# Turning normed head outputs from float32r copies, one step later in the program

## The chip, the cores and the metric

The kernel runs on one core of one Trainium2 chip. A core has TensorE (matrix products; PE in the profile, its weight loads PEld), VectorE (DVE), ScalarE (ACT), GpSimd (POOL) and SyncE (SP). POOL and SP do little here but issue transfers (DMA); each has a queue and issues in order. The metric is device time in microseconds (us) of one execution, as the median of several.

## The reference, cut to what matters

The model is a trunk of two layers over 256 latent and 256 context tokens. Layer 0 has an mLSTM mixer with 4 heads, layer 1 a latent attention; each is followed by a gated convolutional FFN. The change lies in the mixer of layer 0. Its last step norms each head by itself and multiplies by the output matrix:

```python
def out(h_in, s):
    Bq, T, _ = h_in.shape
    o = jax.nn.sigmoid(h_in @ w_og).reshape(Bq, T, M_HEADS, M_DV)
    hsum = o * s.transpose(0, 2, 1, 3).astype(h_in.dtype)
    return _head_rms_norm(hsum, norm_g) @ w_out
```

Here `s` is the output of the two-way scan, per head 512 tokens by 512 columns. The kernel computes the scan of a head in closed form: a matrix W of decay weights (exponentials of gate sums plus a mask) times the scores q k, normed by row, and then times the values.

## The kernel before

All products that matter are made in float32r from split operands: a number is a high part (rounded to float32r) and a low part (the rest), and `mm3` (L427 on) issues three matmuls, high x high (L430), high x low (L433) and low x high (L434), of 128x128 weights and up to 512 columns. Weights stream from DRAM: SP loads a `raw` tile, ACT casts it (L345), DVE makes the low part (L368); three `w` buffers are in turn.

The mixer goes over the heads h = 0 to 3. In each turn `w_qk(h)` projects q and k of head h on TensorE: 4 output tiles, each of two weight units, 24 matmuls a unit, 192 in all. Beside it run *generators*, pieces of Python that emit some instructions at each step; after each unit two steps are taken (`tick`). For h of 2 and 3 these are, one after the other, `post(h - 2)` and `head(h - 1)`:

- `head` loads two gate rows spread over all partitions (`aB`, two transfers on POOL), issues two transfers that start the sums of FFN weights (`t4d`), adds the mask (`Am`, DVE, L1050), and in three groups makes W: exponentials on ACT (L1087), products with the scores on DVE (L1088), norming (L1094 to L1105). Then TensorE turns W (`PT`, 12 transposes, L1118), and ACT and DVE split the result.
- `post` norms the finished output `oh` of the head two before (tiles `tt`): squares on ACT (L1188), root, four multiplications on DVE (L1192). Then TensorE turns them: 16 transposes of 128x128 against the identity, in float32 (`hnT`, L1198), and ACT (L1205) and DVE (L1206) make the split `hn` that the output product reads.

After the projection `av` multiplies the turned W by the values, and `s_mm` makes the next scores. `v_load` loads values (`vr`) and output gates (`oh`) of the head on POOL. The output product `outmm` of the first tokens runs beside `head(3)` and `post(2)`.

The generators set only which instruction is emitted when, and so the place of each tile in its pool and the issue order of POOL's transfers. A scheduler then orders the instructions of each engine by priority and estimated readiness; a tile's wait for its buffer is put in as a semaphore. Tiles of 2 KB a partition share one pool (`s2`) of 15 buffers: `aB`, `Am`, W, `vr`, `oh` and, newly, `rr` are among them.

Of the kernel before, what the change touches and what calls it, by code (L numbers as in the profile page):

```python
# [7 lines left out]
F32 = mybir.dt.float32  # L8
F32R = mybir.dt.float32r
I32 = mybir.dt.int32  # L10
AF = mybir.ActivationFunctionType
ALU = mybir.AluOpType
# [21 lines left out]
NB, NRAW, NU, NS = 3, 3, 31, 15  # L34
# [366 lines left out]
class K:  # L401
# [73 lines left out]
    def setup(self):  # L475
        nc, p = self.nc, self.pool
        a = self.a
        self.sm = p.tile([128, a["sm"].shape[1]], F32, name="sm")
        self.sm0 = p.tile([128, NSM0], F32, name="sm0")
        jp = p.tile([128, 128], I32, tag="s2", name="jp", bufs=NS)  # L480
        nc.gpsimd.iota(jp, pattern=[[1, 128]], base=0, channel_multiplier=-1)
        self.jp = jp
        self.ident = p.tile([128, 128], F32, name="ident")
        self.mask = p.tile([128, 2, 128], F32, name="mask")
        self.k1 = p.tile([128, 1], F32, name="k1")
        nc.vector.memset(self.k1, 1.0)
        self.zero = p.tile([128, 512], F32R, tag="s2", name="zero", bufs=NS)
        nc.vector.memset(self.zero.bitcast(F32), 0.0)
        self.keps = p.tile([128, 1], F32, name="keps")
        nc.vector.memset(self.keps, EPS)  # L490
        self.cond = p.tile([128, 8, 32], F32, tag="s2", name="cond", bufs=NS)
        nc.gpsimd.memset(self.cond, 0.0)
        self.mod0 = p.tile([128, 2, 8, 2], F32, name="mod0")
        self.modc = {(0, c): self.mod0[:, c] for c in range(2)}
        self.gd = {}
        self.adav = p.tile([128, 32], F32, name="adav")
        nc.vector.memset(self.adav, 0.0)
        for l in range(2):
            for c in (3, 4) if l == 0 else (0, 1, 3, 4):
                self.modc[l, c] = p.tile([128, 8, 2], F32, name="mod%d%d" % (l, c))  # L500
            for c in (2, 5):
                self.gd[l, c] = self.dr.tile([2, D], F32, name="gd%d%d" % (l, c))
# [102 lines left out]
    def start_up(self):  # L605
# [47 lines left out]
        with self.tc.manual_schedule(engines={e.PE, e.DVE, e.Activation}):  # L653
            for _ in range(WARM):
                nc.tensor.matmul(idle, self.zero[:, 0:128], self.zero, start=True, stop=True)
            for step in STEPS:
                op, n = step[0], [int(x) for x in step[1:]]
                g = n[0]
                if op == "Q":
                    nc.scalar.activation(self.cond[:, :, 0:2], self.smc("cond").rearrange("p (a b) -> p a b", b=2),  # L660
                                         AF.Silu)
                    nc.vector.tensor_scalar(self.ident, self.jp, 0.0, None, op0=ALU.is_equal)
                    b1 = self.smc("ada_b")[:, 8:16]
                    nc.vector.tensor_scalar(b1, b1, 1.0, None, op0=ALU.add)
                elif op == "M":
                    nc.vector.tensor_scalar(self.mask[:, 0], self.jp, 0.0, NEG, op0=ALU.is_gt, op1=ALU.mult)
                    nc.vector.tensor_scalar(self.mask[:, 1], self.jp, 0.0, NEG, op0=ALU.is_lt, op1=ALU.mult)
                    self.jp = None
                elif op == "I":
                    for _ in range(g):  # L670
                        nc.tensor.matmul(idle, self.zero[:, 0:128], self.zero, start=True, stop=True)
                elif op in "Aab":
                    if g not in rows:
                        rows[g] = self.ps("adar")
                    self.ada_mm(rows[g], [(x, raw["a%d%d" % (g, x)]) for x in {"A": (0, 1), "a": (0,), "b": (1,)}[op]])
                elif op == "C":
                    adas[g] = self.ada_copy(rows[g])
                elif op == "T":
                    self.ada_T(rows[g], adas[g])
                elif op == "O":  # L680
                    self.ada_cols(g, rows[g])
                elif op == "E":
                    self.mod_tile(g)
                elif op == "H":
                    h = hT[g] = self.u("hT")
                    self.split(h[:, 0, :], h[:, 1, :], self.xT[g])
                elif op == "e":
                    h = hT[g] = self.u("hT")
                    x, (c, l) = self.xT[g], (slice(0, 256), slice(256, 512))
                    sh, sc = self.modc[0, 0][:, g], self.modc[0, 1][:, g]  # L690
                    nc.vector.tensor_scalar(x[:, c], x[:, c], sc[:, 1:2], sh[:, 1:2], op0=ALU.mult, op1=ALU.add)
                    nc.scalar.activation(h[:, 0, l], x[:, l], AF.Identity, bias=sh[:, 0:1], scale=sc[:, 0:1])
                    nc.vector.tensor_copy(h[:, 0, c], x[:, c])
                elif op == "l":
                    nc.vector.tensor_scalar(x[:, l], x[:, l], sc[:, 0:1], sh[:, 0:1], op0=ALU.mult, op1=ALU.add)
                    nc.vector.tensor_sub(h[:, 1], x, h[:, 0])
                elif op in "WwvyzKkU":
                    if op == "U":
                        g = "u"
                        raw["wu"] = raw["u0"]  # L700
                    if g not in w:
                        w[g] = [self.pool.tile([128, CW], F32R, tag="u", name="w0", bufs=NU) for _ in range(2)]
                    c = slice(256, nw) if op in "yz" else slice(0, 256 if op in "wv" else 768 if op == "U" else nw if g < 2 else 512)
                    hi, lo, src = w[g][0][:, c], w[g][1][:, c], raw["w%s" % g][:, c]
                    if op == "w":
                        nc.vector.tensor_copy(hi, src)
                    elif op in "WyKU":
                        nc.scalar.copy(hi, src)
                    if op in "WvzkU":
                        nc.vector.tensor_sub(lo, src, hi)  # L710
                else:
                    k, m = n
                    if m not in ps:
                        ps[m] = self.ps("up")
                    wk, o = (w["u"], k - 2) if m == 4 and k > 1 else (w[k], m)
                    c = slice(o * 128, (o + 1) * 128)
                    for i, j in {"V": ((0, 0), (0, 1), (1, 0)), "P": ((0, 0),), "L": ((1, 0),), "R": ((0, 1),)}[op]:
                        nc.tensor.matmul(ps[m], wk[i][:, c], hT[k][:, j], start=made[m] == 0, stop=made[m] == 23)  # L718
                        made[m] += 1
# [460 lines left out]
        self.PT = self.vh = self.oh = None  # L1180
        return r

    def post(self, h, tt):
        nc = self.nc
        ss = self.tiny(4, "ss")
        jk = self.s2("jk")
        for t in range(4):
            nc.scalar.activation(jk, tt[t], AF.Square, accum_out=ss[:, t:t + 1])  # L1188
        nc.scalar.activation(ss, ss, AF.Sqrt, bias=self.keps, scale=1.0 / 512.0)
        nc.vector.reciprocal(ss, ss)  # L1190
        for t in range(4):
            nc.vector.tensor_scalar(tt[t], tt[t], ss[:, t:t + 1], None, op0=ALU.mult)  # L1192
        yield
        g = self.smc("mng")
        for e in range(4):
            pt = self.ps("hnT")
            for t in (2, 0, 1, 3):
                q = nc.tensor.transpose(pt[:, t * 128:(t + 1) * 128], tt[t][:, e * 128:(e + 1) * 128], self.ident)  # L1198
                if e or t != 2:
                    self.behind(q, [lead])  # L1200
                else:
                    lead = q
            k = h * 4 + e
            u = self.u("hn")
            nc.scalar.activation(u[:, 0], pt, AF.Copy, scale=g[:, k:k + 1])  # L1205
            nc.vector.scalar_tensor_tensor(u[:, 1], pt, g[:, k:k + 1], u[:, 0], op0=ALU.mult, op1=ALU.subtract)  # L1206
            self.hn[k] = u
        yield


    def bcast(self, row, name):
        ts = []
# [969 lines left out]
def build(tc, off, a, out):  # L2182
    es = ExitStack()
    with es:
        k = K(tc, es, off, a)
        nc = k.nc
# [16 lines left out]
        for h in range(H0):  # L2203
# [1 line left out]
            if h == 0:  # L2205
                gens.append(k.gate_chain())
            if h >= 2:
                gens.append(k.post(h - 2, tt))
            if h >= 1:
                gens.append(k.head(h - 1, S))  # L2210
            k.bg = gens
            k.w_qk(h, 2, (lambda: k.v_load(h - 1)) if h >= 1 else None)
# [4 lines left out]
        k.xc = None  # L2217
        hn = lambda i: (k.hn[i][:, 0], k.hn[i][:, 1])
        pc = k.acc4()
        k.bg = [k.head(3, S, True), k.post(2, tt)]  # L2220
        vs = k.v_steps(3)
        for i in range(8):
            k.outmm("mout", range(i, i + 1), hn, pc, 0, 16, 2, n2=ADA_M)
            next(vs, None)
        k.drain()
        tt = k.av(3)
        k.bg = [k.post(3, tt)]
        k.outmm("mout", range(8, 12), hn, pc, 0, 16, 1, n2=ADA_M)
        k.drain()
        tokr = a["tok"].rearrange("(t p) d -> t p d", p=128)  # L2230
# [132 lines left out]
```

## Time and profile before

| | us |
|---|---|
| median of 3 runs | 1347.13 (1346.78 to 1347.27) |
| profiled execution, span from first to last instruction | 1345.3 |
| what lies around the span, against the median | 1.8 |
| TensorE busy | 1334.9 |
| DVE busy | 1059.0 |
| ACT busy | 711.7 |
| first of the two changed stretches: matmuls of `w_qk(2)` from | 458.2 |
| second: matmuls of `w_qk(3)`, its hnT at | 524.25 |

A row of the timeline gives the start, the duration, engine, line, operation and tiles (out<-in); a bracket at the end gives the idle time before it and who ended it. On TensorE the records of neighbouring matmuls overlap, so its pace is read from starts. The granted TensorE clock is 0.998 of full speed over the span.

### The profile page before, as it was taken

To read this page: it belongs to the slowest core of one execution; us is meant where nothing else is said; L and a number is where in the kernel's file an instruction comes from. 1 tells how busy PE (TensorE), PEld (TensorE's weight loads), DVE (VectorE), ACT (ScalarE), POOL (GpSimd) and SP (SyncE) were. 2 spreads that over 40 slices of the span, in tenths; PEclk is the share of its full clock that TensorE was granted. 3 is DMA by queue.
4 is the path that set the end of the run, shared out by engine and by line. 5 is a ranking of instruction groups with operands and counts; after the bars stand their busy time and mean duration, and the time that the engine had idled before them with its cause. 6 is when DMAs were issued, how large, how long until landed. Compare 5 with 4: busy or idle time off the path is not lost.

```text
span 1345.3 us, 18750 instructions
## 1 busy us (share of the span) xinstructions
PE 1334.9 (99%) x6659; PEld 1120.2 (83%) x6659; DVE 1059.0 (79%) x1745; ACT 711.7 (53%) x1252; POOL 141.5 (11%) x236
## 2 busy tenths in 40 slices
PE   9999999999999999999999999999999999999997
PEld 5777888888888888888898888888888998988886
DVE  4798656678688696897979977758899889898874
ACT  4765444445744546474644334333566767676660
POOL 0222000011101011020002011111000002000100
PEclk9999999999999999999999999999999999999999
DMA  9988848889686384776628989967866437376750
GB/s 364 330 277 279 281 163 248 233 272 307 235 281 230 102 255 149 228 292 222 215 86 261 328 260 286 282 181 184 300 223 194 157 104 219 127 212 189 263 189 32
DMA packets 99885, 304.02 MB, mean 226 GB/s; under 512 B 12312, under 2 KB 25112, under 8 KB 99712
## 3 DMA queue, kind: packets, MB, share of 16 engines
q1 hardware_dynamic: 62992, 218.65, 48.6%
q0 software_dynamic: 26000, 66.75, 17.9%
q10 hardware_dynamic: 10800, 17.44, 3.6%
q8 instruction: 52, 0.85, 0.3%
q14 instruction: 41, 0.34, 0.1%
HBM read 272.21 MB, written 42.12 MB: 234 GB/s over the span
## 4 chain that ended last, share of the span: by engine, by line
PE 97%; DMA 1%; DVE 1%; ACT 0%; issue 0%; SPq 0%; DVEq 0%; ACTq 0%
PE fin L1503 8%; PE tok L430 6%; PE tok L434 6%; PE tok L433 6%; PE fin L433 6%; PE fin L434 6%; PE y L433 6%; PE fin L430 6%; PE y L434 6%; PE y L430 6%; PE qk L430 4%; PE qk L433 4%; PE qk L434 4%; PE up L718 2%; PE up L430 2%; PE up L434 1%
## 5 line engine op out<-in xcount | busy, mean ns | idle before, releaser
L368 DVE TENSOR_TENSOR w<-raw,w 128x1024 fp32r<-128x1024 f32 (+2 forms) x286 | 343.2, 1203 | 131.9 <-ACT w L345 129.7
L345 ACT CAST w<-raw 128x1024 fp32r<-128x1024 f32 (+2 forms) x286 | 296.2, 1037 | 282.4 <-PE tok L434 77.8
L544 DVE SCALAR_TENSOR_TENSOR junk<-ar,bc 128x1024 f32<-128x1024 f32 x128 | 156.1, 1219 | 5.2 <-ACT bc L586 2.3
L433 PE MATMUL fin<-h,w 128*128 128x512 f32 (+1 forms) x370 | 139.6, 377 | 0.0
L430 PE MATMUL fin<-h,w 128*128 128x512 f32 (+1 forms) x370 | 139.5, 377 | 0.0
L434 PE MATMUL fin<-h,w 128*128 128x512 f32 (+1 forms) x370 | 139.3, 377 | 0.0
L1503 PE MATMUL fin<-h,w 128*128 128x512 f32 (+1 forms) x636 | 111.1, 337 | 0.0
L1503 PEld LDWEIGHTS fin<-h,w 128*128 128x128 f32 x636 | 97.6, 190 | 13.2
L430 PE MATMUL qk<-xc,w 128*128 128x512 f32 x256 | 100.2, 391 | 0.0
L434 PE MATMUL qk<-xc,w 128*128 128x512 f32 x256 | 99.8, 390 | 0.0
L433 PE MATMUL qk<-xc,w 128*128 128x512 f32 x256 | 99.6, 389 | 0.0
L433 PEld LDWEIGHTS fin<-h,w 128*128 128x128 f32 x370 | 69.6, 188 | 13.0
L430 PEld LDWEIGHTS fin<-h,w 128*128 128x128 f32 x370 | 69.6, 188 | 12.9
L434 PEld LDWEIGHTS fin<-h,w 128*128 128x128 f32 x370 | 69.6, 188 | 12.6
L434 PEld LDWEIGHTS qk<-xc,w 128*128 128x128 f32 x256 | 48.0, 188 | 10.1
L430 PEld LDWEIGHTS qk<-xc,w 128*128 128x128 f32 x256 | 48.1, 188 | 9.8
L433 PEld LDWEIGHTS qk<-xc,w 128*128 128x128 f32 x256 | 48.1, 188 | 9.8
L430 PE MATMUL tok<-w,hT 128*128 128x512 f32 x128 | 49.9, 390 | 0.0
L433 PE MATMUL tok<-w,hT 128*128 128x512 f32 x128 | 49.8, 389 | 0.0
L434 PE MATMUL tok<-w,hT 128*128 128x512 f32 x128 | 49.8, 389 | 0.0
L735 ACT ACTIVATE fg<-fg 128x512 f32<-128x512 f32 (+1 forms) x44 | 23.1, 525 | 50.0 <-DVE fg L733 43.9
L368 DVE TENSOR_TENSOR wu<-raw,wu 128x1024 fp32r<-128x1024 f32 (+1 forms) x37 | 43.8, 1203 | 3.5 <-ACT wu L345 3.2
(486 smaller groups left out, 3125.7 us busy)
## 6 DMA issues: line engine op xcount, KB each, us to landing
raw<-in_ws SPq DMA_DIRECT2D x282, 512.0 KB, 4.5
ar<-in_adaT SPq DMA_DIRECT2D x80, 512.0 KB, 6.0
t4d<-in_ws POOLq DMA_DIRECT2D x20, 512.0 KB, 9.1
adaw<-in_ada SPq DMA_DIRECT2D x16, 512.0 KB, 8.0
zr<-fd ACTq DMA_DIRECT2D x33, 128.0 KB, 4.6
xmd<-xr POOLq DMA_DIRECT2D x16, 256.0 KB, 4.4
xcd<-cv POOLq DMA_DIRECT2D x16, 256.0 KB, 4.9
xs<-xmd POOLq DMA_DIRECT2D x16, 256.0 KB, 6.0
```

The costliest lines, as they stand in the source:

```text
L345: self.cast = k.nc.scalar.copy(h[:, :cols], src)
L368: i = self.k.nc.vector.tensor_sub(l[:, :n], src, h[:, :n])
L430: q = mm(out, w[0], x[0], start=start, stop=False, skip_group_check=on)
L433: mm(out, w[0], x[1], start=False, stop=False, skip_group_check=on)
L434: mm(out, w[1], x[0], start=False, stop=stop, skip_group_check=on)
L544: nc.vector.scalar_tensor_tensor(o, w, 1.0, self.bc[j], op0=ALU.mult, op1=ALU.mult, accum_out=col[:, k, j:j + 1])
L718: nc.tensor.matmul(ps[m], wk[i][:, c], hT[k][:, j], start=made[m] == 0, stop=made[m] == 23)
L735: nc.scalar.activation(tmp[:, :n], tmp[:, :n], AF.Silu)
L1503: self.nc.tensor.matmul(ps[:, 0:256] if x else ps, w[x][:, k * 128:(k + 1) * 128], h[:, 0:256] if x else h, start=i == 0 and not k0, stop= ...
```

## The change

For heads 0 and 1 (`post(0)` beside `w_qk(2)`, `post(1)` beside `w_qk(3)`) each normed tile is copied, as it is, by a transfer on POOL's queue into a float32r tile `rr`; the 16 transposes then read `rr` against an identity in float32r and write float32r. `post` has one more empty step before its transposes, for heads 2 and 3 too, which keep the float32 transposes. `around` interleaves the two generators: the norm and the copies of `post`, then the first part of `head` (`aB`, `t4d`, `Am`), then the transposes of `post`, then the rest of `head`.

```diff
+        self.identr = p.tile([128, 128], F32R, name="identr")
...
+                    nc.vector.tensor_scalar(self.identr, self.jp, 0.0, None, op0=ALU.is_equal)
...
-    def post(self, h, tt):
+    def post(self, h, tt, copy=True):
...
+        rr = []
         for t in range(4):
             nc.vector.tensor_scalar(tt[t], tt[t], ss[:, t:t + 1], None, op0=ALU.mult)
+            if copy:
+                r = self.pool.tile([128, 512], F32R, tag="s2", name="rr", bufs=NS)
+                nc.gpsimd.dma_start(r.bitcast(F32), tt[t])
+                rr.append(r)
+        src, ident, dt = (rr, self.identr, F32R) if copy else (tt, self.ident, F32)
+        yield
         yield
...
-                q = nc.tensor.transpose(pt[:, t * 128:(t + 1) * 128], tt[t][:, e * 128:(e + 1) * 128], self.ident)
+                q = nc.tensor.transpose(pt[:, t * 128:(t + 1) * 128].bitcast(dt), src[t][:, e * 128:(e + 1) * 128], ident)
...
+    def around(self, post, head):
+
+        next(post)
+        yield
+        next(head)
+        yield
+        yield from post
+        yield from head
...
             if h >= 2:
-                gens.append(k.post(h - 2, tt))
-            if h >= 1:
+                gens.append(k.around(k.post(h - 2, tt), k.head(h - 1, S)))
+            elif h >= 1:
                 gens.append(k.head(h - 1, S))
...
-    k.bg = [k.head(3, S, True), k.post(2, tt)]
+    k.bg = [k.head(3, S, True), k.post(2, tt, False)]
...
-        k.bg = [k.post(3, tt)]
+        k.bg = [k.post(3, tt, False)]
```

On three engines the order moves. Line numbers of the new kernel are higher by 1 to 18; the buffer numbers behind a name differ between the two.

POOL's queue, from the gates (`oh`) of head 0 to those of head 1. Before:

```order
L1139 DMA oh<-od 128x512 x4
L1045 DMA aB_3990<-ad 128x512
L1045 DMA aB_3991<-ad 128x512
L1662 DMA t4d<-in_ws 16x8192 x2
L1133 DMA vr<-vd 128x512 x4
L1139 DMA oh<-od 128x512 x4
```

Now:

```order
L1141 DMA oh<-od 128x512 x4
L1198 DMA rr<-oh 128x512 x4
L1047 DMA aB_3931<-ad 128x512
L1047 DMA aB_3932<-ad 128x512
L1680 DMA t4d<-in_ws 16x8192 x2
L1135 DMA vr<-vd 128x512 x4
L1141 DMA oh<-od 128x512 x4
```

The four copies stand ahead of the `aB` and `t4d` of head 1.

DVE at the norm of head 0, beside the second weight unit of `w_qk(2)`. Before:

```order
L1050 TENSOR_TENSOR Am_3996<-aB_3990,mask 128x512
L1050 TENSOR_TENSOR Am_3997<-aB_3991,mask 128x512
L1190 RECIPROCAL ss<-ss 128x4
L1192 TENSOR_SCALAR oh<-oh,ss 128x512 x4
L1088 SCALAR_TENSOR_TENSOR W_4042,den<-W_4042,S 128x128
L368 TENSOR_TENSOR w<-raw,w 128x1024
L1206 SCALAR_TENSOR_TENSOR hn<-hnT,sm,hn 128x512 x4
L1088 SCALAR_TENSOR_TENSOR W_4043,den<-W_4043,S 128x256
```

Now:

```order
L1192 RECIPROCAL ss<-ss 128x4
L1195 TENSOR_SCALAR oh<-oh,ss 128x512 x4
L368 TENSOR_TENSOR w<-raw,w 128x1024
L545 SCALAR_TENSOR_TENSOR junk,adav<-ar,bc 128x1024 x2
L1052 TENSOR_TENSOR Am_3937<-aB_3931,mask 128x512
L368 TENSOR_TENSOR w<-raw,w 128x1024
L1052 TENSOR_TENSOR Am_3938<-aB_3932,mask 128x512
L1215 SCALAR_TENSOR_TENSOR hn<-hnT,sm,hn 128x512 x4
L445 TENSOR_TENSOR qk<-qk 128x512
L1090 SCALAR_TENSOR_TENSOR W_4052,den<-W_4052,S 128x128
```

`Am`, which reads `aB`, went from ahead of the norm to behind two products of the modulation (`junk`), with a weight split, `hn` and a `qk` split between it and the first W.

TensorE after 120 of the 192 matmuls of `w_qk(2)`. Before:

```order
L1118 MATMUL PT<-ident,W_4042 128x128
L1118 MATMUL PT<-ident,W 128x128 x2
L1118 MATMUL PT<-ident,W_4064 128x128 x2
L1118 MATMUL PT<-ident,W 128x128 x2
L1118 MATMUL PT<-ident,W_4064 128x128 x2
L430 MATMUL qk<-xc,w 128x512
```

Now:

```order
L1120 MATMUL PT<-ident,W_4052 128x128
L430 MATMUL qk<-xc,w 128x512
L433 MATMUL qk<-xc,w 128x512
L434 MATMUL qk<-xc,w 128x512
L430 MATMUL qk<-xc,w 128x512
L433 MATMUL qk<-xc,w 128x512
L1120 MATMUL PT<-ident,W 128x128 x2
L1120 MATMUL PT<-ident,W_4074 128x128 x2
L1120 MATMUL PT<-ident,W 128x128 x2
L1120 MATMUL PT<-ident,W_4074 128x128 x2
L434 MATMUL qk<-xc,w 128x512
```

Eight of the 12 transposes of W stand five matmuls behind the first four. The 16 transposes hnT stood after 30 matmuls of `w_qk(2)` and stand after 48. The same moves are in `w_qk(3)`. In the output product the 16 transposes of `post(2)` stand 12 matmuls later.

## Prediction

> **What bounds the kernel now.** I read the page first: its busy shares and the chain that ended last.
>
> ```profile
> span 1345.3 us, 18750 instructions
> PE 1334.9 (99%) x6659; PEld 1120.2 (83%) x6659; DVE 1059.0 (79%) x1745; ACT 711.7 (53%) x1252; POOL 141.5 (11%) x236
> PE 97%; DMA 1%; DVE 1%; ACT 0%; issue 0%; SPq 0%; DVEq 0%; ACTq 0%
> ```
>
> TensorE is busy for 1334.9 of 1345.3 us and is 97% of the chain. So a microsecond taken from TensorE is a microsecond of the kernel, and so is every one that it waits; there are only 10.4 us of gaps to win back. Next, the line that the change touches, and TensorE's own sequence in the first of the two stretches that change (projection of head 2, with `post(0)` and `head(1)` beside it).
>
> ```profile
> L1198 PE MATMUL hnT<-ident,oh x64: 270/273/328, 465.1 to 616.9; 128*128 128x128 f32 x64
>   DVE oh L1192: 0.6, 2
> ```
>
> ```profile
> 458.20 0.39 PE L430 MATMUL qk<-xc,w 128*128 128x512 f32 x1
> ...
> 464.77 0.39 PE L434 MATMUL qk<-xc,w 128*128 128x512 f32 x1
> 465.06 2.03 PE L1198 MATMUL hnT<-ident,oh 128*128 128x128 f32 x16
> 466.85 0.48 PE L430 MATMUL qk<-xc,w 128*128 128x512 f32 x1
> 467.17 0.40 PE L433 MATMUL qk<-xc,w 128*128 128x512 f32 x1
> ...
> 487.39 1.47 PE L1118 MATMUL PT<-ident,W 128*128 128x128 f32 x12
> 488.62 0.47 PE L430 MATMUL qk<-xc,w 128*128 128x512 f32 x1
> ...
> 489.85 0.40 PE L434 MATMUL qk<-xc,w 128*128 128x512 f32 x1
> ```
>
> Starts count here, since the records overlap. Thirty matmuls start from 458.20 to 464.77: 6.57 / 29 = 0.227 us each. The 16 turns (hnT) cost what is left between 464.77 and 467.17 after two such steps: 2.40 - 0.45 = 1.95 us. The wait for `oh` (0.6 us at two places, counted on the weight load) is mostly inside it. At 487.39 the `PT` turns follow without a stall: so the head's weights W were ready just in time or earlier. DVE tells how much earlier.
>
> ```profile
> 454.83 1.28 DVE L1050 TENSOR_TENSOR Am<-aB,mask 128x512 f32<-128x512 f32 x2
> 463.73 1.68 DVE L1192 TENSOR_SCALAR oh<-oh,ss 128x512 f32<-128x512 f32 x4
> 466.17 1.23 DVE L368 TENSOR_TENSOR w<-raw,w 128x1024 fp32r<-128x1024 f32 x1 [0.56 <-ACT w L345]
> 467.31 2.72 DVE L1206 SCALAR_TENSOR_TENSOR hn<-hnT,sm,hn 128x512 fp32r<-128x512 f32 x4
> 469.95 0.42 DVE L1088 SCALAR_TENSOR_TENSOR W<-W,S 128x256 f32<-128x256 f32 x1
> ...
> 472.23 0.69 DVE L445 TENSOR_TENSOR qk<-qk 128x512 fp32r<-128x512 f32 x1
> 472.83 0.17 DVE L1098 RECIPROCAL R<-R 128x4 f32<-128x4 f32 x1
> ...
> 480.06 1.22 DVE L544 SCALAR_TENSOR_TENSOR junk<-ar,bc 128x1024 f32<-128x1024 f32 x1
> ...
> 482.47 0.16 DVE L1098 RECIPROCAL R<-R 128x2 f32<-128x2 f32 x1
> ...
> 484.79 0.74 DVE L1105 SCALAR_TENSOR_TENSOR W<-W,R 128x512 f32<-128x512 f32 x1
> 485.45 1.22 DVE L368 TENSOR_TENSOR w<-raw,w 128x1024 fp32r<-128x1024 f32 x1
> ```
>
> The last W is done by about 485.5 and the turns start at 487.39: 1.9 us of room, with DVE working without a gap from 466.17 on. This chain is what stands next in line behind TensorE. It starts early because its rows `aB` come long before:
>
> ```profile
> 418.19 0.54 POOL L1045 DMA_DIRECT2D aB<-ad  x1 [7.19 <-DVE junk L544]
> 422.28 0.54 POOL L1045 DMA_DIRECT2D aB<-ad  x1 [3.55 <-PE PT L1118]
> ...
> 467.18 1.65 POOL L1133 DMA_DIRECT2D vr<-vd  x3 [43.37 <-PE hnT L1198]
> ```
>
> POOL's queue issued both `aB` transfers 32 us before Am read them, and then stood at `vr` for 43.37 us.
>
> **The change, part by part.** *The turns.* The trace has no 128-column float32r matmul. Bound from above: the float32r matmul of 256 columns, which loads the same 128x128 weights.
>
> ```profile
> 1068.40 0.28 PE L433 MATMUL kn<-ckT,wu 128*128 128x256 f32 x1
> 1068.52 0.28 PE L434 MATMUL kn<-ckT,wu 128*128 128x256 f32 x1
> ```
>
> It starts every 0.12 us, so 16 turns cost at most 1.92 us. From below: 256 columns less (0.227 to 0.12) save 0.107, 128 less save 0.054, so 0.066 each and 1.06 us. I take the middle, 0.093 each, 1.5 us: 0.45 us saved a head, between 0.03 and 0.89. The weight load may be what decides: "TensorE: Matmul & The Clock Gate" of the Trainium skill (section "Weight-path perf modes — Fast Weight Load (FWL) and DoubleRow") lets 128 weights of any type but FP32 load fast. By that rule the lower end would hold, and the sum would be 0.9 us lower if nothing else waited; no row here shows a load of that kind by itself.
>
> *Where they stand.* The turns now come 18 matmuls later, at 464.77 + 0.23 + 18 x 0.227 = 469.1. Their copies are issued as DVE norms each tile: the first is normed by 464.15, POOL needs 0.55 us for each issue (1.65 for three), so the four go out from 464.2 to 466.4, the last starting at 465.85. The nearest rows for landing are a store from SBUF on the same queue (x3d, first line below) and the loads vr (second):
>
> ```profile
> DMA to landing us min/median/max: 2.3/3.3/4.1
> DMA to landing us min/median/max: 3.0/4.7/9.0
> ```
>
> From 2.3 to 4.7 us: the last copy is there between 468.2 and 470.6, and TensorE asks for it with the fourth turn at 469.4. A stall of 0 to 1.2 us; I take none (3.3), as the DMA engines are empty then:
>
> ```profile
> 464.90:467.20 2.30, 2.30 (x20) 2.01 (x19) 1.74 (x5) 2.30 (x5) 0.03 (x1) 1.00 0.00 0
> ```
>
> (DMA share 0.00 and 0 GB/s, at the row's end.)
>
> *POOL's order.* This is the step that decides. `aB` of the next head stood ahead of everything of `post`; now it is queued behind the four copies, and those wait for the norm. So `aB` goes out at 466.4 and no longer at 418. It lands after (the 8 transfers of aB):
>
> ```profile
> DMA to landing us min/median/max: 4.5/6.6/7.3
> ```
>
> It runs behind 1 MB of copies, but on engines that were empty; I take the middle of the bounds, 5.9, so `aB` lands at 472.3 (470.9 to 473.7). By "DMA: Bandwidth & Descriptors" of the Trainium skill (section "Anatomy of one DMA — SWDGE (gpsimd) path") a transfer takes about 2.0 us plus its bytes over 436 GB/s; the estimate for copies and first `aB` together (1.25 MB) would be 5.0 us from 464.2, that is 469.2. The row's least, 4.5 for 256 KB alone, disagrees with it.
>
> *The chain behind it.* DVE's new order from the landing on: Am 0.64, a weight split 1.14, Am 0.64, four hn 2.64 (467.31 to 469.95), a qk split 0.60: 5.66 us. Then the head's own work, which took 469.95 to 485.45 = 15.50 us before; in the new order it holds two junk products less (480.06 to 482.47, 2.41 us), one qk split less (0.60) and one small W more (0.2): 12.7 us. So the last W is ready at 472.3 + 5.66 + 12.7 = 490.7. ACT does not set it:
>
> ```profile
> 463.50 1.28 ACT L1087 ACT_TABLE_LOAD   x1
> ...
> 466.04 2.41 ACT L1205 ACTIVATE hn<-hnT,sm 128x512 fp32r<-128x512 f32 x4
> ...
> 468.33 0.41 ACT L1087 ACTIVATE W<-Am,gcol 128x128 f32<-128x128 f32 x1
> ...
> 471.47 0.58 ACT L444 CAST qk<-qk 128x512 fp32r<-128x512 f32 x1
> ```
>
> From about 470.5 it does hn (2.41), qk (0.5) and the table load (1.28) and reaches the exponentials at 474.7, ten of which take 3.1 us (468.33 to 471.47); DVE wants the first product at 478.0.
>
> *What TensorE does meanwhile.* It reaches the second group of `PT`, which now stands five matmuls after the first, at 487.39 - 0.45 + 0.6 (four turns of 0.11, and the change of kind) + 5 x 0.227 = 488.7 and waits for W until 490.7: 2.0 us. Per head: -0.45 for the turns, +0.15 for one more change between turns and matmuls (466.85 to 467.17 is 0.09 over a step, 464.77 to 465.06 is 0.06 over one), +2.0 wait: **+1.7 us**. The second stretch has the same rows 59.2 us later,
>
> ```profile
> 524.25 2.03 PE L1198 MATMUL hnT<-ident,oh 128*128 128x128 f32 x16
> ```
>
> so twice: **+3.4 us**. The saving at the turns is worth nothing as long as that wait lasts: TensorE only arrives earlier.
>
> *Costs of nothing.* `identr` is one small DVE operation beside the start-up matmuls. The two `t4d` transfers move with `aB` and are read only after the first FFN. `vr` comes out after the turns as before, and is read from 494.85 on; `oh` goes out when the exponentials end, about 481, and is read at 506.61: more than 15 us of room each.
>
> ```profile
> 494.85 2.18 ACT L444 CAST v<-vr 128x512 fp32r<-128x512 f32 x4
> ...
> 506.61 0.69 DVE L1178 TENSOR_TENSOR oh<-av,oh 128x512 f32<-128x512 f32 x1
> ```
>
> The weight splits keep their room: the unit split behind the first Am is ready at 474.1 and TensorE takes it after 98 matmuls, at 482. `post(2)` has its turns 12 matmuls (2.7 us) later, and 42 matmuls stand between them and the first reader of hn.
>
> **Rivals.** *Late, but hidden* (25%): `aB` lands after 4.5 us, at 470.9, the chain ends at 489.3. With the middle price of a turn that is +0.3 a head, with the cheapest the same, since the chain, not TensorE, sets it: +0.6 us, 1347.7. For it: empty DMA engines; against it: half of the eight `aB` took 6.6 us or more.
>
> *The turns decide* (12%): `aB` lands as fast as the quickest store, 2.3 us, at 468.7, and the chain is over by 487.1, before TensorE; then only the turns count: 2 x (-0.89 + 0.15) = -1.5, 1345.6, and with the change between kinds free, -1.8. Against it: no `aB` came before 4.5 us. Nothing in the rows lets it win more: faster by 0.2% would need something that I have not seen. The formula from "DMA: Bandwidth & Descriptors" in the Trainium skill, quoted above, speaks for this rival: by it the chain would end at 469.2 + 18.4 = 487.6.
>
> *Late and later* (13%): POOL's issues slip, which ends further on the slow side. The copies are issued just while DVE norms; if POOL can only write them after 465.4, everything from `aB` on moves by 1.2 us, and with 7.3 us to landing the chain ends at 473.7 + 1.2 + 18.4 = 493.3: +4.3 a head, +8.6, 1355.7. The rows leave open whether they can. "SBUF — State Buffer" of the Trainium skill has the rule (section "SBUF: two separate sides", the warning on the "DVE blocks DMA" trap): descriptors of POOL's transfers are not written while DVE runs in a mode with two ports.
>
> *As forecast* (50%).
>
> **How the numbers follow.** The profiled execution has a span of 1345.3 us, the median of the runs is 1347.13, 1.8 us around it; the sum is a difference and goes onto the median: 1347.13 + 3.4 = 1350.5. Its own range goes from 4.9 to 7.3 us for `aB`: 2 x (-1.0 to +1.4) around it, 1348.5 to 1353.3. The range for 8 in 10 takes in the hidden case and most of the worst: 1346.3 to 1354.6. A difference under 0.2% (2.7 us) is about what a measurement cannot tell from none, so slower begins at 1349.8. The forecast is slower in four fifths of its cases (0.41) and the worst always (0.13): 0.54. Same: the rest of the forecast, the hidden case and most of the third: 0.37. Faster: 0.09, for what I have not seen.
>
> **What would show it.** A first `aB` of head 1 issued near 466 and landing near 472; Am behind it; the exponentials at 475; and TensorE idle for about 2 us at `PT`, 125 matmuls into each of the two projections, put down to DVE's W. The copies should land by 469, with no idle time at hnT, and the 16 turns take 1.1 to 1.9 us. No idle time at `PT`, or a last W before 488.7, would make the forecast wrong on the low side; idle time at hnT as well, on the high side.

## The result, and the profile after

| | before | after |
|---|---|---|
| median of 5 runs, us | 1347.25 (1346.78 to 1347.97) | 1356.13 (1355.6 to 1358.11) |
| ratio | | 1.0069 (95% interval 1.0056 to 1.0081) |
| span of the profiled execution, us | 1345.3 | 1354.4 |
| granted TensorE clock over the span | 0.998 | 0.994 |

The changed kernel is 8.9 us slower. I had forecast 3.4 us slower, with a range that ended at 1354.6. The page of the changed kernel, its busy shares and the chain that ended last:

```profile
span 1354.4 us, 18779 instructions
PE 1338.1 (99%) x6659; PEld 1123.1 (83%) x6659; DVE 1059.3 (78%) x1746; ACT 713.6 (53%) x1252; POOL 146.2 (11%) x244
PE 94%; issue 4%; DMA 1%; DVE 0%; POOL 0%; ACT 0%; SPq 0%; DVEq 0%; POOLq 0%
```

TensorE has as many instructions as before, but is busy for 3.2 us more in a span that is 9.1 us longer. So some 6 us are idle time and 3 us are slower work. The waits of TensorE over both changed stretches name one place:

```profile
PE hnT L1207 <- DMA rr<-oh: 5.8, 4, 1.7
```

Four waits, two in each stretch, 5.8 us in all, at the turns hnT, for the copies. At PT, where I had put the wait, there is none. TensorE's timeline in the first stretch (start, duration, operation; the bracket is the idle time before it and who ended it):

```profile
468.84 0.39 PE L434 MATMUL qk<-xc,w 128*128 128x512 f32 x1
470.76 0.42 PE L1207 MATMUL hnT<-identr,rr 128*128 128x128 f32 x3 [1.53 <-DMA rr<-oh]
472.91 1.89 PE L1207 MATMUL hnT<-identr,rr 128*128 128x128 f32 x13 [1.73 <-DMA rr<-oh]
474.59 0.76 PE L430 MATMUL qk<-xc,w 128*128 128x512 f32 x1
475.15 0.63 PE L433 MATMUL qk<-xc,w 128*128 128x512 f32 x1
475.57 0.63 PE L434 MATMUL qk<-xc,w 128*128 128x512 f32 x1
...
493.20 0.60 PE L1120 MATMUL PT<-ident,W 128*128 128x128 f32 x4
...
494.81 1.04 PE L1120 MATMUL PT<-ident,W 128*128 128x128 f32 x8
```

TensorE asks for the first turn at 468.84 + 0.23 = 469.07, as forecast (469.1), but the copy it needs first is there only at 470.76 and the last one at 472.91. And behind the turns the matmuls start 0.42 us apart where 0.227 is normal. The windows say why (columns: busy time of the five engines, granted TensorE clock, DMA share, GB/s):

```profile
464.00:470.00 6.00, 5.23 (x24) 3.99 (x22) 4.90 (x9) 1.90 (x4) 4.38 (x8) 1.00 0.64 186
470.00:473.00 3.00, 0.52 (x4) 0.41 (x4) 0.00 (x0) 0.31 (x1) 0.00 (x0) 0.91 1.00 354
473.00:475.00 2.00, 2.00 (x14) 2.00 (x15) 0.00 (x0) 1.69 (x3) 0.16 (x1) 0.50 1.17 369
475.00:479.00 4.00, 4.00 (x11) 3.03 (x11) 3.75 (x5) 3.97 (x10) 1.50 (x3) 0.50 0.90 316
479.00:483.00 4.00, 4.00 (x18) 3.32 (x17) 3.97 (x19) 2.54 (x8) 0.54 (x1) 0.97 0.53 202
```

From 473 to 479 the clock is at half; 11 matmuls start in 4 us instead of 17.6. The first group of PT stood at 487.39 before and stands at 493.20: this stretch lost 5.8 us. (At the first PT of the second stretch, 546.57 before and 556.22 now, 9.7 us are lost.) From 469.07 to the first matmul behind the turns (474.59) it takes 5.52 us; without any wait that is 1.3 us (see "direct" below), so 4.2 us are lost there. From 474.59 to 493.20 there are 72 matmuls: 18.61 us where 72 x 0.227 = 16.34, another 2.3 us. The second stretch has the same two waits, shorter (1.46 and 1.10 us).

What the copies met. The rows are POOL's and SyncE's issues, then DVE's weight split and first product of the modulation, its first Am and its last W:

```profile
464.77 2.33 POOL L1198 DMA_DIRECT2D rr<-oh  x4 [53.79 <-DVE oh L1195]
467.09 1.08 POOL L1047 DMA_DIRECT2D aB<-ad  x2
468.14 1.01 POOL L1680 DMA_DIRECT2D t4d<-in_ws  x2
...
466.55 0.33 SPq L308 DMA_DIRECT2D raw<-in_ws  x1
467.69 0.33 SPq L568 DMA_DIRECT2D ar<-in_adaT  x1
...
465.30 1.22 DVE L368 TENSOR_TENSOR w<-raw,w 128x1024 fp32r<-128x1024 f32 x1
466.44 1.22 DVE L545 SCALAR_TENSOR_TENSOR junk<-ar,bc 128x1024 f32<-128x1024 f32 x1
...
475.12 0.69 DVE L1052 TENSOR_TENSOR Am<-aB,mask 128x512 f32<-128x512 f32 x1 [6.13 <-DMA aB<-ad]
...
493.67 0.75 DVE L1107 SCALAR_TENSOR_TENSOR W<-W,R 128x512 f32<-128x512 f32 x1
```

SyncE's raw goes out as the weight split ends (466.52), and ar as the product ends (467.66): each waits for a buffer that DVE still reads. The copies took 2.4/4.0/6.3 us to land (least, median, most), aB took up to 9.4. DVE idles for 6.13 us for aB, and the last W is done at 494.42, in time for a TensorE that comes late itself: the second group of PT starts at 494.81.

### The profile page after: what moved, and what is told of

It reads as the page before. It is cut to its first block, busy times and chain, and to the rows that moved or that the text cites. A ratio compares the mean times of both kernels' runs of the same rounds, so it can differ in the third digit from the quotient of the medians.

```text
span 1354.4 us, 18779 instructions
## 1 busy us (share of the span) xinstructions
PE 1338.1 (99%) x6659; PEld 1123.1 (83%) x6659; DVE 1059.3 (78%) x1746; ACT 713.6 (53%) x1252; POOL 146.2 (11%) x244
## 4 chain that ended last, share of the span: by engine, by line
PE 94%; issue 4%; DMA 1%; DVE 0%; POOL 0%; ACT 0%; SPq 0%; DVEq 0%; POOLq 0%
PE fin L1521 8%; PE y L433 6%; PE y L434 6%; PE y L430 6%; PE tok L430 6%; PE tok L434 6%; PE tok L433 6%; PE fin L434 6%; PE fin L433 6%; PE fin L430 6%; PE qk L430 3%; PE qk L433 3%; PE qk L434 3%; PE up L720 2%; PE up L430 1%
## 5 line engine op out<-in xcount | busy, mean ns | idle before, releaser
L430 PE MATMUL qk<-xc,w 128*128 128x512 f32 x256 | 101.7, 397 | 0.0
L434 PE MATMUL qk<-xc,w 128*128 128x512 f32 x256 | 100.9, 394 | 0.0
L433 PE MATMUL qk<-xc,w 128*128 128x512 f32 x256 | 100.8, 394 | 0.0
```

The source lines that it names most:

```text
L430: q = mm(out, w[0], x[0], start=start, stop=False, skip_group_check=on)
L433: mm(out, w[0], x[1], start=False, stop=False, skip_group_check=on)
L434: mm(out, w[1], x[0], start=False, stop=stop, skip_group_check=on)
```

## The experiments

All times are medians, beside runs of the kernel before on the same chip (1346.99 to 1347.18). Line numbers of the experiments differ by a few from those of the change. Each diff is against the changed kernel, or adds to the experiment named with it.

**The order alone.**

```diff
-    k.around(k.post(h - 2, tt), k.head(h - 1, S))
+    k.around(k.post(h - 2, tt, False), k.head(h - 1, S))
```

> The changed kernel's order (the turns after 48 matmuls, the norm ahead of the next head's first part), but no copies: the 16 turns of heads 0 and 1 read the normed tiles in float32 as before. If the copies are what costs (late landing at hnT, or their place ahead of aB on POOL's queue), aB is issued early again, nothing waits at hnT or PT, and the time is that of before within 1.5 us: 1346 to 1349. If the order itself costs (turns later, ACT and DVE work shifted, W late at PT), it stays slow: 1350 to 1356.

Measured: 1347.1, ratio 1.0001 (0.9992 to 1.0010). The new order costs nothing that the interval shows; the whole loss comes with the copies (their landing, or their place ahead of aB). The rows of its turns are needed further down:

```profile
469.23 0.39 PE L434 MATMUL qk<-xc,w 128*128 128x512 f32 x1
469.46 1.91 PE L1207 MATMUL hnT<-ident,oh 128*128 128x128 f32 x16
471.13 0.48 PE L430 MATMUL qk<-xc,w 128*128 128x512 f32 x1
471.44 0.40 PE L433 MATMUL qk<-xc,w 128*128 128x512 f32 x1
```

**aB and t4d first, whole steps exchanged.**

```diff
-        next(post)
-        yield
-        next(head)
-        yield
+        next(head)
+        yield
+        next(post)
+        yield
```

> Copies and float32r turns as in the change, but the first part of the next head (aB, t4d, Am) is issued ahead of the norm and the copies. If the copies are late because aB and t4d crowd the DMA engines just behind them, the copies now land in 2.4 to 3.3 us after their issue, the wait at hnT is 0 to 1 us a head instead of 3.3 and 2.6, the clock does not drop, W is early, and the time is 1345 to 1349. If four copies of 256 KB take 4 to 6 us by themselves, the wait stays at 2 us or more a head and the time is 1351 to 1356; W early changes nothing then.

Measured: 1367.8 (1.0157; 1.0142 to 1.0172). Both expectations missed: the exchange moved the norm as well. On DVE of this kernel:

```profile
466.66 1.22 DVE L545 SCALAR_TENSOR_TENSOR junk<-ar,bc 128x1024 f32<-128x1024 f32 x1
...
469.34 1.68 DVE L1195 TENSOR_SCALAR oh<-oh,ss 128x512 f32<-128x512 f32 x4
```

The norm stands behind a weight split and two products of the modulation, 5.6 us later than in the change (463.71), and the copies with it; TensorE waited 16.5 us at hnT. It says what a late copy costs, and nothing on aB. The run with aB and t4d early, below, leaves the norm in its place.

**The turns later, copies and aB as in the change.**

```diff
         next(head)
         yield
+        next(post)
+        yield
+        next(head)
+        yield
         yield from post
```

> As the change, but the turns stand 24 matmuls (5.4 us) later, after 72, behind the first exponentials of W; POOL's order is that of the change, with aB behind the copies. If the wait at hnT is the whole loss, it is gone (the copies landed by 475, TensorE asks at about 474.7) and the time is 1346 to 1349. If the late aB is a loss of its own that was only hidden behind the wait at hnT, TensorE now reaches PT near 489 and waits for the last W until 492 to 494, 3 to 5 us a head: 1353 to 1358.

Measured: 1360.42 (1.0102; 1.0087 to 1.0117). TensorE's waits over both stretches, and its rows in the first:

```profile
PE PT L1120 <- DVE W L1107: 10.9, 2, 5.5
```

```profile
474.56 1.49 PE L1207 MATMUL hnT<-identr,rr 128*128 128x128 f32 x16
...
486.88 0.60 PE L1120 MATMUL PT<-ident,W 128*128 128x128 f32 x4
```

No wait at hnT any more, and 5.4 to 5.5 us a head at PT, for W. This is the wait of my forecast, at its place, and larger. In the change it is hidden behind the wait at hnT, since TensorE comes 5.8 us later. Here the last W is ready at 495.67, 1.2 us later still. Mending the first wait alone, this way, makes the kernel slower.

**TensorE kept busy in the wait.**

```diff
             pt = self.ps("hnT")
+            if copy and e == 0:
+                w, x = self.xc[0][:, 0, 0:128], self.xc[0][:, 0, 0:512]
+                for i in range(14):
+                    q = nc.tensor.matmul(pt, w, x, start=True, stop=True)
```

> As the change, with 14 more matmuls of 512 columns (their results are overwritten by the turns) in front of the first turn of heads 0 and 1: 14 x 0.227 = 3.2 us of TensorE work where it waited 3.3 and 2.6 us. If the half clock behind the wait comes from the idling, the clock stays full, and the first head gains some 2 us, the second some 1.2 less 0.6 that the 14 stick out: 1352.5 to 1354. If the clock drops for another reason (the float32r turns, or chance), nothing is gained: 1356 to 1358.

Measured: 1362.5 (1.0114; 1.0097 to 1.0131). Slower, not faster. Its waits (in an execution of 1365.5 us, the longest of four), and one window behind the turns:

```profile
PE PT L1120 <- DVE W L1107: 7.5, 2, 3.8
```

```profile
475.00:480.00 5.00, 5.00 (x24) 4.13 (x23) 4.78 (x9) 4.09 (x10) 0.95 (x2) 1.00 0.89 338
```

The clock holds at 1.00, as one expectation had it, and so TensorE is at PT early enough to meet the late W: the second cause again. And behind that wait the clock falls after all (0.50 over 495 to 500). What the half clock costs had to be measured where W is early.

**aB and t4d early, nothing else moved.** `head` gets a step of its own that only issues the two transfers.

```diff
+        next(head)
         next(post)
         yield
...
         if not big:
             self.t4_step(2)
+        if early:
+            yield
         Am = [self.s2("Am0"), self.s2("Am1")]
...
```

> As the change, but POOL issues aB and t4d of the next head ahead of the copies (Am, norm, copies and turns keep their places), so W is made in time and the copies run without aB and t4d behind them. If the two transfers crowd the copies, they now land within 3.3 us of their issue, by 470, the wait at hnT is 0 to 1 us a head, the clock holds, and the time is 1346 to 1349. If the copies are slow by themselves, or beside the weight loads alone, 2 to 3 us of waiting a head and some half clock stay: 1351 to 1356.

Measured: 1354.94 (1.0058; 1.0044 to 1.0071). The interval overlaps that of the change. The norm keeps its place, W is early, and yet TensorE waits; the waits, those of the first stretch, and the landing of the copies:

```profile
PE hnT L1209 <- DMA rr<-oh: 5.5, 4, 2.3
```

```profile
472.02 0.51 PE L1209 MATMUL hnT<-identr,rr 128*128 128x128 f32 x4 [2.30 <-DMA rr<-oh]
473.22 1.22 PE L1209 MATMUL hnT<-identr,rr 128*128 128x128 f32 x12 [0.69 <-DMA rr<-oh]
```

```profile
DMA to landing us min/median/max: 2.5/3.7/6.1
```

So aB and t4d behind the copies are not what makes these late.

**t4d early, aB late.** `around` as in the run before; `head` issues t4d in that first step, and aB where the change has it.

```diff
+        if early:
+            self.t4_step(2)
+            yield
         aB = [self.s2("aB0"), self.s2("aB1")]
...
```

> As the change, but only t4d goes out ahead of the copies; aB stays behind them. If t4d's bytes are what holds up both, aB lands by 472 (as I forecast) and the copies by 470: no wait of over 1.5 us at hnT, up to 2.5 us at PT, 1349 to 1353. If t4d does not matter, waits and time stay as in the change: 1355 to 1357.

Measured: 1356.6 (1.0072; 1.0056 to 1.0087), waits of 5.9 us at hnT and 1.4 at PT. The place of t4d makes no difference that the interval shows.

**aB and t4d early, and the turns later.** Both edits together.

> aB and t4d ahead of the copies, and the turns 24 matmuls later. If the two waits (copies at hnT, W at PT) are all that the change costs, none is left, and what remains is the turns' saving of 0.5 us a head: 1345.5 to 1347. If the later turns or the copies' traffic cost something else, 1348 or more.

Measured: 1347.16, ratio 1.0002 (0.9993 to 1.0011). With both waits taken away the loss is gone: those two, with what follows from them, are all of it, to within 1.3 us. The turns' saving does not show. Two waits of 0.7 us at PT are left in the trace, but that is of an execution of 1348.91 us; the ten others took 1347.69 at most.

**No copies, float32r tiles written by VectorE.** The values are rounded on the way, so this is a kernel to measure with, and no replacement.

```diff
-            nc.vector.tensor_scalar(tt[t], tt[t], ss[:, t:t + 1], None, op0=ALU.mult)
             if copy:
                 r = self.pool.tile([128, 512], F32R, tag="s2", name="rr", bufs=NS)
-                nc.gpsimd.dma_start(r.bitcast(F32), tt[t])
+                nc.vector.tensor_scalar(r, tt[t], ss[:, t:t + 1], None, op0=ALU.mult)
                 rr.append(r)
+            else:
+                nc.vector.tensor_scalar(tt[t], tt[t], ss[:, t:t + 1], None, op0=ALU.mult)
```

> No copies at all: VectorE writes the normed values straight into the float32r tiles (rounded to float32r, so the low part of hn is lost for heads 0 and 1), in the place of the norm; the turns are float32r, after 48 matmuls. Without copies nothing waits at hnT and aB is issued early: the turns' saving of 0.5 us a head stands alone, 1345.5 to 1347. If the float32r kind or the place of the turns costs by itself, 1348 or more.

Measured: 1346.41, ratio 0.9994 (0.9985 to 1.0003). It gives the price of the turns at full clock and without a wait:

```profile
468.95 0.39 PE L434 MATMUL qk<-xc,w 128*128 128x512 f32 x1
469.19 1.49 PE L1208 MATMUL hnT<-identr,rr 128*128 128x128 f32 x16
470.51 0.46 PE L430 MATMUL qk<-xc,w 128*128 128x512 f32 x1
470.81 0.39 PE L433 MATMUL qk<-xc,w 128*128 128x512 f32 x1
```

(470.51 - 469.19) / 16 = 0.083 us each. From 468.95 to 470.81, less two steps of 0.227, is 1.41 us, against 1.95 for the float32 turns before, worked out the same way: 0.54 us a head, 1.1 us in all. That is what the change could win at most, less than a measurement tells here. The kind of the turns has only part of it: in the run of the order alone, float32 turns at this place take 471.44 - 469.23 less two steps, 1.76 us, 0.35 more than these. The other 0.19 are mostly the wait for `oh` that the old place had.

**The half clock, with W early.** The 14 matmuls above, now 13, on top of aB and t4d early.

> As the run with aB and t4d ahead of the copies, with 13 matmuls of 512 columns (overwritten by the turns) where TensorE waited for the copies: 13 x 0.227 = 2.95 us against waits of 3.0 and 2.5 us a head. TensorE still cannot turn earlier, so only the half clock can be won: if it comes from the idling, the clock stays at 1.0 behind the turns and some 1.5 to 1.8 us a head are won, 1351 to 1352.5. If it does not, the time stays at 1354.5 to 1356.

Measured: 1352.29 (1.0038; 1.0023 to 1.0053), 2.65 us less than without the fill. The same two windows, first without the fill, then with it (two runs):

```profile
475.00:479.00 4.00, 4.00 (x13) 3.14 (x12) 4.00 (x9) 4.00 (x10) 1.18 (x3) 0.63 0.65 197
```

```profile
475.00:479.00 4.00, 4.00 (x20) 3.30 (x19) 4.00 (x12) 4.00 (x11) 2.31 (x6) 1.00 0.88 269
```

Clock 0.63 and 13 matmuls, against 1.00 and 20. TensorE cannot turn any earlier in this run (its last group of turns in the first stretch starts at 473.20, without the fill at 473.22), so the 2.65 us are what idling cost through the clock: 1.3 us a head.

**Which other bytes.** First, on top of aB and t4d early, the loads of the modulation (`ar`) moved two weight units back:

```diff
-                self.tick(nt, ADA_Q)
+                self.tick(nt, ADA_Q * (0 if h >= 2 and j == 0 else 2 if h >= 2 and j == 2 else 1))
```

> As the run with aB and t4d ahead, but the products of the modulation (junk), and with them the loads ar of 512 KB each, are taken out of the first two weight units of the projections of heads 2 and 3 and done two units later. If the copies are late because they share the DMA engines with raw and ar (2.1 MB at some 290 GB/s), 0.5 MB less lets the last copy land up to 1.7 us earlier: waits of 0.5 to 1.5 us a head, no half clock, 1348 to 1351. If four copies of 256 KB take their 4 us by themselves, the waits stay and the time is 1354 to 1356.

Measured: 1353.96 (1.0053; 1.0037 to 1.0069), waits of 5.0 us at hnT. A little less waiting in the first stretch (1.46 + 0.73 us instead of 2.30 + 0.69), not the recovery that one expectation had: ar still went out at 470.40, and raw, at 466.90, was still beside the copies. The four executions took 1355.6 and 1356.2 us at a clock of 0.996 and 0.995 over the span, and 1352.1 and 1352.3 at 0.998; the trace is of the first. So whether the clock falls behind waits of this size differs from one execution to the next.

Half of the copies, on top of aB and t4d early:

```diff
+            if copy and t % 2 == 0:
+                r = self.pool.tile([128, 512], F32R, tag="s2", name="rr", bufs=NS)
+                nc.vector.tensor_scalar(r, tt[t], ss[:, t:t + 1], None, op0=ALU.mult)
+                rr.append(r)
+                continue
```

> As the run with aB and t4d ahead, but only the second and fourth tile are copied; the first and third are written as float32r by VectorE itself (rounded, their low part is lost). Half of the copied bytes: if bytes on the engines are what delays the copies, the last one lands 1.5 us or more earlier, the waits at hnT shrink to 0.5 to 1.5 us a head without half clock, 1347 to 1350. If a copy has a fixed delay of 4 to 5 us behind its issue, the last still lands late and the time is 1352 to 1355.

Measured: 1345.98, ratio 0.9993 (0.9983 to 1.0002), no wait at hnT. Two copies are in time where four are not.

Then the weight load held back until the copies are in, again with aB and t4d early (the edit also takes `post`'s first step ahead of the projection's first load, which leaves the norm where it was, at 464.20):

```diff
+        if copy:
+            hold = self.dr.tile([128, 4], F32, name="hold%d" % h)
+            self.hold = [self.nc.sync.dma_start(hold[:, t:t + 1], rr[t].bitcast(F32)[:, 0:1]) for t in (2, 0, 1, 3)]
...
-            k.nc.sync.dma_start(t[:, :cols], self.ws[n, :, :cols])
+            i = k.nc.sync.dma_start(t[:, :cols], self.ws[n, :, :cols])
+            k.behind(i, k.hold)
+            k.hold = []
...
```

> As the run with aB and t4d ahead of the copies, but SyncE's queue issues four transfers of 512 bytes that read the copies, ahead of the next weight load (raw), so that raw goes out only when the last copy has landed (ar behind the first). If the copies are late because raw and ar share the engines with them, 1 MB alone takes some 3 us from 466.6: all landed by 469.6 to 470, waits of 0 to 0.8 us a head, no half clock, 1346 to 1349. If POOL's queue moves them slowly even alone, they land at 472 or later as before and the time is 1353 to 1356.

Measured: 1348.51 (1.0011; 1.0001 to 1.0020). Waits of TensorE, landing of the copies, and SyncE's queue:

```profile
PE hnT L1215 <- DMA rr<-oh: 1.4, 2, 0.9
```

```profile
DMA to landing us min/median/max: 2.5/2.8/3.7
```

```profile
468.18 0.40 SPq L570 DMA_DIRECT2D ar<-in_adaT  x1
470.17 1.28 SPq L1207 DMA_DIRECT2D hold<-rr  x3
471.54 9.14 SPq L308 DMA_DIRECT2D raw<-in_ws  x3
```

With raw out of the way the slowest copy lands in 3.7 us instead of 6.1, and 6.4 us of the 7.8 us of loss are gone. The copies were issued at the same time in both (from 465.26 and 465.27), and ar too (468.18 and 468.19). So the copies were late because they shared the DMA engines with SyncE's loads, and raw is the one that counts.

**Another queue.** Against the change, only the engine that issues the copies:

```diff
-                nc.gpsimd.dma_start(r.bitcast(F32), tt[t])
+                nc.scalar.dma_start(r.bitcast(F32), tt[t])
```

> As the change, but the four copies are issued on ScalarE's queue, which waits for nothing else at that time; POOL can issue aB and t4d early. If POOL's issuing (0.55 us a copy, and what follows it) is what makes the copies late, they land in 2 to 3 us and the time is 1346 to 1349. If the engines' bytes are what counts, the wait at hnT stays at 2 to 3 us a head, as with aB and t4d ahead on POOL: 1352 to 1356.

Measured: 1346.88, ratio 0.9996 (0.9987 to 1.0006).

> The kernel with the copies on ScalarE's queue once more, with more rounds, since under one microsecond is asked: if nothing but the turns changes, 16 turns and their changes of kind cost 0.5 us a head less, 1346.1 against 1347.1 of the kernel before, a ratio of 0.9992; if ScalarE's four issues (2.4 us of its time) or the later place take it back, 1.0000.

Measured: 1346.75, ratio 0.9998 (0.9989 to 1.0006). No time can be told from that of before; whether the 1.1 us are in it stays open. The landing of the copies in this second run:

```profile
DMA to landing us min/median/max: 2.3/2.4/2.4
```

Nothing waits at hnT or PT. How early the bytes move shows in the windows of the first run on this queue, where DVE's norm began at 463.27, and then in those of the change, where it began at 463.71:

```profile
464.50:465.00 0.50, 0.50 (x4) 0.38 (x4) 0.50 (x3) 0.00 (x0) 0.00 (x0) 1.00 0.07 29
465.00:465.50 0.50, 0.50 (x4) 0.42 (x3) 0.50 (x1) 0.00 (x0) 0.00 (x0) 1.00 1.03 385
```

```profile
465.50:466.00 0.50, 0.50 (x4) 0.42 (x3) 0.50 (x1) 0.00 (x0) 0.50 (x2) 1.00 0.00 0
466.00:466.50 0.50, 0.50 (x4) 0.42 (x3) 0.50 (x2) 0.00 (x0) 0.50 (x2) 1.00 0.89 344
```

From ScalarE's queue they move 1.7 us after the norm begins, over a microsecond ahead of raw (issued at 466.11); from POOL's 2.3 us after it, half a microsecond ahead of raw's issue (466.55). By queue, the trace of that first run shows all of the copies' 1.05 MB moved from 465 to 468 and nothing of SyncE's; raw follows with 0.32 MB from 468 to 469. On POOL's queue, with aB and t4d early, 0.71 MB had moved by 469; the other 0.34 MB took until 473, beside 0.94 MB of SyncE's. And with the copies on ScalarE's queue POOL is free to issue aB early (at 438). Both waits are gone with one word.

| step | us | against before |
|---|---|---|
| the change | 1356.13 | +8.9 |
| aB and t4d early | 1354.94 | +7.8 |
| and TensorE kept busy in the wait | 1352.29 | +5.1 |
| instead of that, raw held back | 1348.51 | +1.4 |
| the change with ScalarE's queue | 1346.75 to 1346.88 | -0.3 to -0.4 |
| the change with later turns | 1360.42 | +13.4 |

## Why the prediction was wrong

- *The turns.* Right: 0.093 us forecast, 0.083 measured, so the lower end, 0.066, did not hold. With the change between kinds 0.54 us a head are saved, where I had 0.30; 0.35 of that is the kind, and the rest mostly the wait for `oh` that I had counted into the old price.
- *The copies at hnT: the step that failed.* "A stall of 0 to 1.2 us; I take none (3.3), as the DMA engines are empty then". TensorE waited 3.3 us in the first stretch and 2.6 in the second. The row that I took this from showed the kernel before, and ended at 467.20, while I had the copies on their way until 469. There, SyncE issued the next raw at 467.42, just behind the row, and ar at 477.43. In the change a weight split and two products of the modulation follow the norm on DVE; these set buffers free, and SyncE issued raw at 466.55 and ar at 467.69, with the copies still on their way. The last copy was there at 472.9, not by 469.4. Held back, raw gives 6.4 us of time back, which shows it; raw had come only 0.9 us sooner than before. The bound itself was too low as well: 4.7 us is the median of the row of vr, whose most is 9.0, and 6.3 us occurred.
- *The clock.* Not in my sum at all. Waits of 1.53 and 1.73 us, with three turns between them, brought the clock to half for 6.8 us in the first stretch; the second had 3.4 us of it. The fill put it at 1.3 us a head, in a kernel that had 3.4 us in each. In the change itself it need not cost that: one of the five executions kept a clock of 0.998 over its span and took 1355.95, about as long as the others. Presumably a TensorE that comes earlier meets the late W there, as in the run with the fill; no trace of that execution shows it.
- *aB behind the copies.* The mechanism was right and its size too small: issued at 467.09 (466.4 forecast), Am at 475.12 (472.3), last W at 494.42 (490.7). 0.7 us of that is POOL, 2.1 us the landing (8.0 us, not 5.9), 0.9 us the chain. Alone it costs some 5.4 us at PT a head and not 2.0, as the run with later turns shows, though W is later there by 1.2 us. In the change itself it costs nothing, as another wait comes before it.
- *The sum.* I had +1.7 a head; the trace has 5.8 in the first: by the parts above about 4.2 at the turns and 2.3 behind them, less the 0.5 saved, which comes to 6.0.
- *The rivals.* "Late, but hidden" and "The turns decide" fell. "Late and later" was near in its time (1355.7) and came true for W (494.4, it had 493.3), but not as the cause of this kernel's loss. Its trigger was borne out for the first copy: the issue began at 464.77 but took 0.74 us, not 0.54, and ended 0.12 us behind the norm. So it did in both stretches of all ten runs with four copies on POOL (0.12 us each time). The other three followed at 0.54 each, so that aB moved by 0.7 us and not by 1.2. The estimate by the formula, copies and first aB by 469.2, was 6 us too early: Am began at 475.12.
- I had named "idle time at hnT as well" as what would make the forecast wrong on the high side. It came, and stood in place of the wait at PT, not beside it.

## What to carry to other kernels

A free resource in the profile of before is free for the work that runs there before: when a step moves, look up which buffers the instructions beside it release, and which loads start from that, before a landing time is taken from an empty engine; and a row that shows it empty has to reach to the end of the flight. Of two late inputs only the later wait shows, so a mended wait must be priced against the next one. And a transfer on a chain of a few microseconds belongs on a queue with nothing behind it that is needed, and that starts quickly.

## What the hardware showed that I had not expected

*The clock falls after a short wait.* With waits of 2.3 and 0.69 us around four turns the granted clock fell to half, 0.63 over 475 to 479; with one wait in each stretch, of 0.6 and 0.9 us (raw held back), it held at 1.00. After the wait of 5.3 us at PT, with later turns, it was 0.50 over 495 to 500. The length of the wait alone does not decide: 1.46 and 0.73 us in one stretch were enough (ar later), while a single wait of 2.4 us (t4d early, second stretch) left it at 1.00. What the windows' clocks lack to 1.00 says how long it was at half: in the change 6.8 us in the first stretch and 3.4 in the second (0.79 over 535 to 543); with aB and t4d early 3.4 in each. The Trainium skill has the rule ("TensorE: Matmul & The Clock Gate", section "Part 1: The HAM clock gate (the "warmup" mystery)"): after at least one idle window of about 3.4 us the clock is halved, and at least one busy window of about 3.4 us brings it back. The lengths at half, one or two times 3.4 us, agree with it. The fall came with less than 3.4 us of waiting, and with turns in between, so the window need not be wholly idle; how idle it has to be, no run here shows.

*Transfers of different queues share the engines.* The same four copies took up to 6.3 us from POOL's queue and 2.4 us from ScalarE's, where their bytes began 0.6 us sooner behind the norm. That each engine takes turns between the two kinds of queue is stated in the Trainium skill ("DMA: Bandwidth & Descriptors", section "SWDGE vs HWDGE vs iDMA"); the run with raw held back agrees with it (3.7 us at most instead of 6.1). The turns were not even ones: from 469 to 473, with copies on POOL's queue pending (aB and t4d early), SyncE's queue moved 0.94 MB and POOL's 0.34. From ScalarE's queue the copies hardly met raw, so the head start is enough to explain their 2.4 us. How they would fare from there beside a load, no run here shows.
